# x's transposes shared between DMA and TensorE, and gate and Fourier columns in four equal blocks with the layouts' weighting on VectorE

## The chip, the cores and the metric

The kernel runs on one core of a Trainium2 chip. The metric is device time in microseconds (us), the median of three runs. The profile is of one further execution.

## The reference, cut to what matters

One encoder layer over x (2048 tokens, 1024 columns): RMSNorm, one projection `hn @ w_in` to 6144 columns, split into Fourier columns u_f (512) and their gate g_f (512), queries, keys and values of 24 heads (3 x 1536), and the attention's gate g_a (512).

```python
f = fft2(u_f over sequence and head dim).real @ w_fourier        # per group of 64 columns
y_f = f * silu(g_f)
# three dilated layouts, 8 heads each: o_c and lse_c for layout c
alpha = softmax(stack(lses), axis=0)
y_a = sum(alpha[..., None] * stack(outs), axis=0) * silu(g_a)
y = x + concat([y_f, y_a]) @ w_out
```

q and k are RMS-normed per head, with gains q_norm_w and k_norm_w. The last three lines' weighting (alpha) is "the layouts' weighting" below.

## The kernel before, in words

**Precision.** Each operand of a projection is split into a high and a low fp16 part (index j or l is 0 or 1), and three products of parts are summed, so a product over K = 1024 takes 8 x 3 = 24 matmuls. `xT[:, j, k, token]` holds x transposed, part j.

**The stream of items.** `body` builds a list of items; each is one PSUM tile filled by 24 matmuls. 192 items (`inproj`, L314) are 12 units (layout c, slot pair) times 16 token tiles, with 384 columns of q, k and v. Then come 32 channel items (`chan`, L568, moving 512 tokens: 16 of Fourier gate, 16 of u_f), and 32 token items (`tok`, L582, 256 gate columns for 128 tokens). One loop over i issues item i in slices, and between the slices everything else of that step, by hand: the attention block scheduled for it, the norm of q and k, the weights of the next block, and the output step of the item before (`prev()`). Every engine runs its queue in order, so the place in this loop is the order of work on each engine.

**Weights of a block** (`w_prep`, L254). A block is up to 384 columns. Per block VectorE takes eight maxima (L262), TensorE turns the per-partition maximum round (L268, out 1 x 128), VectorE makes two scale factors on one partition (L270 to L274), TensorE spreads them over 128 partitions (L276, out 128 x 2), and then ScalarE writes the high parts (L291) and VectorE the low parts (L293). There are 17 blocks: 12 units and, by `TSEG`, five in the tail of 384, 384, 256, 256 and 256 columns. `plan` says how many steps of the next block's preparation go into each item.

**The start.** x is loaded by 16 row tiles of 512 KB on SyncE's queue (SP), six buffers. ScalarE sums squares (L191), VectorE takes the reciprocal root (`rsqrt_g`, L103 to L110), ScalarE writes the high part (`x_hi`, L214), VectorE the low part (`x_lo`, L221). Tile 0 is transposed on TensorE (L228), and ScalarE copies the PSUM tiles (L233). Tiles 1 to 15 are transposed by two DMAs each, on SP (`x_dt`, L237). Item 0 of unit 0 needs tile 0, item t needs tile t. Between these, `setup2a` loads both gain tables for all 128 partitions by broadcast (768 KB each, L145 and L146), and `setup2b` makes the combined gains on 128 partitions (GpSimd L158 and L174, VectorE L161 to L171).

**The layouts' weighting** (`og_w`, `og_mul`, `og_add`). The attention writes its outputs with their maxima and sums to DRAM (tile O). For each of 16 groups q of 256 tokens and 256 columns, a load brings all three layouts (792 KB, L634), GpSimd copies maxima and sums out (L647, L648), VectorE makes the weights in eight small steps (L650 to L669) with one exponential on ScalarE (L657), GpSimd multiplies (128 x 1536, L674), and VectorE adds the three layouts (L681, L683). `ga_out` then applies silu (ScalarE L591 and L592, VectorE L593) and multiplies (L693); a token item thus needs its group's sum. The loads start 12 items ahead of the first token item, and the steps run in pace with the token items, one group for two items. ScalarE's silu frees the PSUM tile of a token item, and needs a buffer `ye`, of which there are two, freed by L693.

**Fourier columns** (`u_out`). After every fourth u_f item VectorE and GpSimd fold the sequence into four half-length arrays F (VectorE L619, L622, L623; GpSimd L621, L626, L627).

**The end** (`tail_`). Transposed products with the Fourier map (L746), DFT matmuls (L776), and the output projection (L885) in 16 row tiles. It starts when the last token item's matmuls are done.

Of the kernel before, what the change touches and what calls it, by code (L numbers as in the profile page):

```python
# [23 lines left out]
HD = 64  # L24
# [64 lines left out]
class Kernel:  # L89
# [35 lines left out]
    def setup(self):  # L125
        nc, a, cst = self.nc, self.a, self.cst
        self.idf = cst.tile([128, 128], F32, name="idf")
        make_identity(nc, self.idf)
        self.idh = cst.tile([128, 128], F16, name="idh")
        nc.vector.tensor_copy(self.idh, self.idf)  # L130
        self.ones = cst.tile([1, 128], F32, name="ones")
        nc.vector.memset(self.ones, 1.0)
        self.nw = cst.tile([128, KT], F32, name="nw")
        nc.scalar.dma_start(self.nw, a["norm_w"].rearrange("(k p) -> p k", p=128), allow_slow_non_contiguous=True)
        self.IS = cst.tile([128, 2, 3, 2, 2], F32, name="IS")
        self.dist = self.btp.tile([128, 640], BF16, name="dist")
        self.kf = self.btp.tile([128, 24, HD], F32, name="kf")
        self.bsc = cst.tile([128, 24], F32, name="bsc")
        self.om = cst.tile([128, 24], F32, name="om")
        self.nom = cst.tile([128, 24], F32, name="nom")  # L140

    def setup2a(self):
        nc, a = self.nc, self.a
        kq = self.kq[:, 0].rearrange("p k n -> p (k n)").bitcast(F32).rearrange("p (h d) -> p h d", d=HD)
        nc.sync.dma_start(self.kf, bcast(a["k_norm_w"], 1536))  # L145
        nc.sync.dma_start(kq, bcast(a["q_norm_w"], 1536))  # L146
        nc.sync.dma_start(self.bsc, bcast(a["slopes"], 24))
        nc.sync.dma_start(self.dist, a["dist"])
        self.kqv = kq

    def setup2b(self):
        V = self.nc.vector
        kq = self.kqv
        mx = self.sm.tile([128, 24], F32, name="kmx", bufs=1)
        inv = self.sm.tile([128, 24], F32, name="kinv", bufs=1)
        for i in range(3):
            h = slice(8 * i, 8 * i + 8)
            self.nc.gpsimd.tensor_tensor(self.kf[:, h], self.kf[:, h], kq[:, h], OP.mult)  # L158
        for i in range(3):
            h = slice(8 * i, 8 * i + 8)  # L160
            V.tensor_reduce(mx[:, h], self.kf[:, h], AX.X, OP.max, apply_absolute_value=True)  # L161
            yield
        V.tensor_scalar(mx, mx, 2.0 ** -13, None, op0=OP.max)
        yield
        self.pow2(mx, self.om, inv)
        yield
        V.tensor_scalar(inv, inv, 8.0, None, op0=OP.mult)
        V.tensor_scalar(self.om, self.om, 1.0 / 128, None, op0=OP.mult)
        yield
        V.scalar_tensor_tensor(self.bsc, self.bsc, 8.0, inv, op0=OP.mult, op1=OP.mult)  # L170
        V.tensor_scalar(self.nom, self.om, -1.0, None, op0=OP.mult)  # L171
        for i in range(3):
            h = slice(8 * i, 8 * i + 8)
            self.nc.gpsimd.tensor_tensor(self.kf[:, h], self.kf[:, h], inv[:, h].unsqueeze(2).to_broadcast([128, 8, HD]), OP.mult)  # L174
            yield
# [40 lines left out]
    def x_lo(self, r):  # L216
# [4 lines left out]
        nc.vector.scalar_tensor_tensor(hl[1], t, ri, hl[0], op0=OP.mult, op1=OP.subtract)  # L221
# [9 lines left out]
    def x_ev(self, r, j):  # L231
        E = self.nc.scalar.copy if j or r == 0 else self.nc.vector.tensor_copy
        E(self.xT[:, j, :, r * 128:(r + 1) * 128], self.XP.pop((r, j)))  # L233
# [20 lines left out]
    def w_prep(self, u, nxt=False):  # L254
# [4 lines left out]
        am8 = self.sm.tile([128, KT + 1], F32, name="am8", bufs=2)  # L259
        am = am8[:, KT:KT + 1]  # L260
# [4 lines left out]
        V.tensor_reduce(am, am8[:, :KT], AX.X, OP.max, apply_absolute_value=True)  # L265
# [3 lines left out]
        sc = self.sm.tile([1, 4], F32, name="sc", bufs=2)  # L269
        V.tensor_reduce(sc[:, 2:3], pm[0:1, :128], AX.X, OP.max)  # L270
        V.tensor_scalar(sc[:, 2:3], sc[:, 2:3], 2.0 ** -58, None, op0=OP.max)
        self.pow2(sc[:, 2:3], sc[:, 1:2], sc[:, 0:1])
        V.tensor_scalar(sc[:, 0:1], sc[:, 0:1], 8.0, None, op0=OP.mult)
        V.tensor_scalar(sc[:, 1:2], sc[:, 1:2], 1.0 / 16, None, op0=OP.mult)  # L274
        yield
        nc.tensor.matmul(pm[:, 128:130], self.ones, sc[:, 0:2], start=True, stop=True)  # L276
        sb = self.sm.tile([128, 4], F32, name="scb", tag="scb", bufs=17)
        nws = self.sm.tile([128, KT], F32, name="nws", bufs=2)
        V.tensor_copy(sb[:, 0:2], pm[:, 128:130])
        V.tensor_scalar(nws, self.nw, sb[:, 0:1], None, op0=OP.mult)  # L280
# [294 lines left out]
    def tok(self, u, r):  # L575
# [4 lines left out]
        for k in range(KT):  # L580
            for j, l in ((0, 0), (0, 1), (1, 0)):
                nc.tensor.matmul(ps[:, :256], self.xT[:, j, k, r * 128:r * 128 + 128], wh[:, l, k, :256],  # L582
                                 start=n == 0, stop=n == 23)
                n += 1
                if n % 12 == 0:
                    yield
        self.PS[u, r] = ps
# [7 lines left out]
    def gf_out(self, u, col, ct, ch):  # L595
# [4 lines left out]
        else:  # L600
            t = self.gp.tile([128, 2, 6, UW], F32, name="go", tag="ot", bufs=4).rearrange("p r a w -> p (r a w)")
            o, z = t[:, 0:512], t[:, 512:1024]
# [3 lines left out]
    def u_out(self, u, col, ct, ch):  # L606
        nc = self.nc
        V, G = nc.vector, nc.gpsimd
# [12 lines left out]
        G.tensor_tensor(O[:, 1:1024], U[:, 1:1024], U[:, 2047:1024:-1], OP.subtract)  # L621
# [15 lines left out]
    def og_w(self, q):  # L637
        nc = self.nc
        V, A, G = nc.vector, nc.scalar, nc.gpsimd
        hf, g = divmod(q, 8)  # L640
        ot = self.OT[q]
        T = lambda n, sh: self.sm.tile([128] + sh, F32, name=n, tag=n, bufs=2)
        w, nm, ss = T("cw", [2, 3, 4]), T("cn", [2, 3, 4]), T("cs", [2, 3, 4])
        mn, rc = T("cm", [2, 4]), T("cr", [2, 4])
        fl = lambda x: x.rearrange("p r c (s h) -> p (r c s) h", h=2)
        ov = ot.rearrange("p r a w -> p (r a) w")
        G.tensor_copy(fl(nm), ov[:, :, 130:132])  # L647
        G.tensor_copy(fl(ss), ov[:, :, 128:130])  # L648
# [5 lines left out]
        V.tensor_tensor(w, mn.unsqueeze(2).to_broadcast([128, 2, 3, 4]), nm, OP.subtract)  # L654
        yield
        yield
# [6 lines left out]
        V.tensor_tensor(w, w, iv.unsqueeze(1).to_broadcast([128, 2, 3, 4]), OP.mult)  # L663
# [5 lines left out]
        V.tensor_tensor(w, w, rc.unsqueeze(2).to_broadcast([128, 2, 3, 4]), OP.mult)  # L669
        self.OW[q] = fl(w)  # L670

    def og_mul(self, q):
        O = self.OT[q].rearrange("p r a w -> p (r a) w")[:, :, 0:128].rearrange("p a (h d) -> p a h d", d=HD)
        self.nc.gpsimd.tensor_tensor(O, O, self.OW.pop(q).unsqueeze(3).to_broadcast([128, 12, 2, HD]), OP.mult)  # L674

    def og_add(self, q):
        V = self.nc.vector
        y = self.gp.tile([128, 2, 256], F32, name="yo", tag="yo", bufs=3)
        yv = y.rearrange("p r (s w) -> p r s w", s=2)
        ov = self.OT.pop(q).rearrange("p r (c s) w -> p r c s w", c=3)  # L680
        V.tensor_tensor(yv, ov[:, :, 0, :, 0:128], ov[:, :, 1, :, 0:128], OP.add)  # L681
        yield
        V.tensor_tensor(yv, yv, ov[:, :, 2, :, 0:128], OP.add)  # L683
        self.YO[q] = y

    def ga_out(self, u, hf, r):
        nc = self.nc
        ps = self.PS.pop((u, r))
        q, j = divmod(hf * NT + r, 2)
        y = self.YO[q][:, j]  # L690
        e = self.gp.tile([128, 2, 256], F32, name="ye", tag="ye", bufs=2)
        self.silu(e[:, 0], ps[:, :256], self.W[u][1], e[:, 0], e[:, 1])
        nc.vector.tensor_tensor(y, y, e[:, 0], OP.mult)  # L693
# [200 lines left out]
    TSEG = [[(512, 384)], [(896, 128), (0, 256)], [(256, 256)], [(GAOFF, 256)], [(GAOFF + 256, 256)]]  # L894

    def body(self):
# [3 lines left out]
        with ExitStack() as ctx:  # L900
# [12 lines left out]
            self.YA = drm.tile([S, 512], F32, name="YA")  # L913
            for d in "W WL WS PS RAW QS QR HL TR ST QW VT BT SB PB PH OB OT DT AT OI MX OW XS XR XH XP YO WR XO".split():
# [5 lines left out]
            self.kq = self.wp.tile([128, 2, KT, 384], F16, name="kq", tag="wh", bufs=2)  # L920
# [9 lines left out]
            self.setup2a()  # L930
# [6 lines left out]
            g0 = self.x_rs(0)  # L937
            go(g0, g0, g0, g0, wg, g0, wg, g0, wg, g0, wg, g0, g0, wg, g0, g0)
            for _ in g0:
# [3 lines left out]
            self.x_ev(0, 0)  # L943
            go(wg, wg, wg, wg)
            self.x_lo(0)
            self.x_load(6)
            go(wg)
            self.x_sq(1)
            self.x_tr(0, 1)
            self.x_ev(0, 1)  # L950
            self.x_sq(2)
            go(wg, wg, wg)
# [287 lines left out]
```

## Time and profile before

| | |
|---|---|
| median of 3 runs | 1478.12 us (1477.78 to 1478.91) |
| profiled execution, its own time | 1476.58 us |
| its span, first to last instruction | 1474.8 us |
| mean granted TensorE clock | 0.988 |
| busy: TensorE, VectorE, ScalarE, GpSimd | 1419.4, 1018.1, 744.4, 540.4 us |

PE is TensorE's matmuls, PEld its weight loads, DVE VectorE, ACT ScalarE, POOL GpSimd, SP SyncE, whose queue issues most DMAs. A row of a group reads: line, engine, operation, output<-input, shapes, xcount | busy us, mean ns of one | idle us of the engine just before them, and what ended that idle time. A row of a window reads: start and end, then for each engine its busy us and its number of instructions, then the granted clock (1.00 is full), the DMA engines' busy share and GB/s.

### The profile page before, as it was taken

Reading aid. Unit: us, or ns where it says so; the run is one execution under the profiler, and the core shown is the slowest. Engines: PE = TensorE matmul, PEld = TensorE weight load, DVE = VectorE, ACT = ScalarE, POOL = GpSimd, SP = SyncE. Lnnn points to the kernel's source line nnn. Section 1 sums busy time; section 2 is a strip of 40 time slices with the busy share of each in tenths; the row PEclk is TensorE's granted clock in tenths of the full one; section 3 lists DMA queues with packets and bytes.
Section 4 is the critical chain, followed back from the end, with each engine's and each line's share of the span. In section 5 each row is a group of like instructions: output and inputs, shape, how many; then the busy total and the mean of one; then the engine's idle time right before and its main releaser. Section 6 shows DMA issues by size and latency. Waiting matters only on the chain.

```text
span 1474.8 us, 27958 instructions
## 1 busy us (share of the span) xinstructions
PE 1419.4 (96%) x9466; PEld 1027.9 (70%) x9466; DVE 1018.1 (69%) x3231; ACT 744.4 (50%) x2119; POOL 540.4 (37%) x659
## 2 busy tenths in 40 slices
PE   5899999999999999999999999999998889999999
PEld 2456666667777676678888888644446777878887
DVE  7777888888887887888877787643369995721111
ACT  5666767676756676666666666452222325310000
POOL 1255444444444444444443334310246450411110
PEclk9999999999999999999999999999998999999999
DMA  8987767676776777686746554543214546243332
GB/s 263 219 180 128 144 126 143 126 139 128 142 125 131 136 128 134 124 145 114 149 99 128 105 127 105 131 114 102 73 44 131 182 134 228 101 139 118 108 107 79
DMA packets 425375, 194.66 MB, mean 132 GB/s; under 512 B 321616, under 2 KB 405776, under 8 KB 424720
## 3 DMA queue, kind: packets, MB, share of 16 engines
q1 hardware_dynamic: 424192, 192.87, 58.0%
q8 instruction: 74, 1.21, 0.4%
q14 instruction: 69, 0.57, 0.1%
q10 hardware_dynamic: 1040, 0.00, 0.0%
HBM read 74.17 MB, written 29.75 MB: 70 GB/s over the span
## 4 chain that ended last, share of the span: by engine, by line
PE 69%; DVE 15%; issue 5%; DMA 5%; POOL 4%; ACT 2%; SPq 1%; POOLq 0%; ACTq 0%; DVEq 0%
PE psq L314 35%; PE py L885 12%; PE psq L568 11%; PE pS L463 2%; DMA st<-hl 2%; PE pf L776 2%; PE po L529 2%; POOL ph L511 2%; DVE yo L681 2%; DVE cm L650 1%; DVE qnt L106 1%; DVE wh L293 1%; PE ptr L746 1%; PE pS L451 1%; PE po L530 1%
## 5 line engine op out<-in xcount | busy, mean ns | idle before, releaser
L314 PE MATMUL psq<-wh,xT 128*128 128x384 f16 x4608 | 797.2, 329 | 14.1 <-DMA xT<-xhl 11.4
L314 PEld LDWEIGHTS <-xT 128*128 128x128 f16 x4608 | 541.2, 119 | 215.9 <-issue 16.9
L499 ACT ACTIVATE P<-pS,ob,om 128x256 f32<-128x256 f32 (+1 forms) x384 | 199.6, 527 | 180.7 <-DVE ob L491 180.1
L511 POOL TENSOR_TENSOR ph<-P,ph 128x512 f16<-128x512 f32 x160 | 188.7, 1180 | 189.6 <-ACT ph L506 178.2
L367 POOL TENSOR_TENSOR qn<-qn,kf 128x128 f32<-128x128 f32 x192 | 90.7, 472 | 309.3 <-DVE qn L366 207.9
L885 PE MATMUL py<-wo,mx 128*128 128x512 f32 x768 | 181.3, 395 | 0.3 <-DVE mx L864 0.3
L481 DVE CUSTOM_DVE_ANT_0 pS<-pS,bt 128x256 f32<-128x256 f32 (+1 forms) x384 | 147.6, 384 | 35.0 <-PE pS L451 23.3
L568 PE MATMUL psq<-xT,wh 128*128 128x512 f16 x768 | 169.4, 379 | 0.0
L885 PEld LDWEIGHTS py<-wo,mx 128*128 128x128 f32 x768 | 143.2, 188 | 32.3 <-DVE mx L864 0.8
L378 POOL TENSOR_TENSOR hl<-qn,hl 128x256 f16<-128x256 f32 x192 | 132.9, 692 | 34.0 <-ACT hl L373 34.0
L568 PEld LDWEIGHTS <-wh 128*128 128x128 f16 x768 | 73.7, 98 | 86.9 <-issue 1.4
L888 DVE TENSOR_TENSOR xo<-xo,py 128x512 f32<-128x512 f32 x32 | 22.0, 688 | 139.1 <-PE py L885 139.1
L540 DVE TENSOR_REDUCE ob<-po 128x128 f32<-128x256 f32 (+1 forms) x160 | 75.1, 470 | 44.1 <-PE po L530 44.0
L582 PE MATMUL psq<-wh,xT 128*128 128x256 f16 x768 | 92.5, 285 | 12.5 <-ACT ye L592 8.6
L373 ACT CAST hl<-qn 128x256 f16<-128x256 f32 x192 | 77.1, 401 | 54.3 <-POOL qn L367 47.6
L293 DVE SCALAR_TENSOR_TENSOR wh<-wr,nws,wh 128x384 f16<-128x384 f32 (+1 forms) x136 | 94.7, 704 | 11.8 <-ACT wh L291 11.8
L506 ACT CAST ph<-P 128x512 f16<-128x512 f32 x160 | 99.1, 619 | 5.1
L582 PEld LDWEIGHTS <-xT 128*128 128x128 f16 x768 | 78.2, 102 | 26.7 <-issue 14.5
L333 ACT CAST vt<-psq 128x128 f16<-128x128 f32 x192 | 51.2, 267 | 66.4 <-PE po L530 66.2
L863 ACT CAST mx<-pya 128x512 fp32r<-128x512 f32 x16 | 9.4, 587 | 148.1 <-issue 124.9
L325 ACT COPY raw<-psq 128x256 f32<-128x256 f32 x192 | 69.5, 362 | 26.3 <-PE psq L314 26.0
L334 DVE TENSOR_TENSOR vt<-psq,vt 128x128 f16<-128x128 f32 x192 | 54.9, 286 | 38.1 <-ACT vt L333 37.8
(153 smaller groups left out, 1887.8 us busy)
## 6 DMA issues: line engine op xcount, KB each, us to landing
wr<-in_w_in_dram SPq DMA_DIRECT2D x104, 192.0 KB, 2.8
ot<-O SPq DMA_DIRECT2D x16, 792.0 KB, 4.8
st<-st SPq DMA_DIRECT2D x96, 128.0 KB, 2.4
xs<-in_x_dram SPq DMA_DIRECT2D x16, 512.0 KB, 4.7
xo<-in_x_dram SPq DMA_DIRECT2D x16, 512.0 KB, 3.5
out_dram<-xo SPq DMA_DIRECT2D x15, 512.0 KB, 2.9
O<-ob SPq DMA_DIRECT2D x108, 66.0 KB, 2.4
O<-ob SPq DMA_DIRECT2D x32, 132.0 KB, 2.6
```

The lines of the kernel that those rows point to most:

```text
L293: V.scalar_tensor_tensor(wh[:, 1, k - 1, :n], wr[k - 1], nws[:, k - 1:k], wh[:, 0, k - 1, :n], op0=OP.mult, op1=OP.subtract)
L314: nc.tensor.matmul(ps[:, :384], self.xtile(j, k, c, t), wh[:, l, k, :384], start=n == 0, stop=n == 23)
L367: G.tensor_tensor(qn[:, 2:4], qn[:, 2:4], self.kf[:, h0:h0 + 2], OP.mult)
L373: self.nc.scalar.copy(hl.rearrange("p a h l d -> p (a h) l d")[:, :, 0], qn)
L378: self.nc.gpsimd.tensor_tensor(hv[:, :, 1], qn, hv[:, :, 0], OP.subtract)
L481: V.tensor_tensor_reduce(out=sS[:, h, cs], in0=ps[:, h, cs], in1=bs, scale=1.0, scalar=-3.0e38, op0=OP.add, op1=OP.max, accum_out=mx[:, e, ...
L499: self.nc.scalar.activation(P[:, h, cs], sS[:, h, cs], AF.Exp, bias=ob[:, e, 130 + h:131 + h], scale=self.om[:, h0 + h:h0 + h + 1], accum_ ...
L506: self.nc.scalar.copy(ph[:, 0], P)
L511: self.nc.gpsimd.tensor_tensor(ph[:, 1], P, ph[:, 0], OP.subtract)
L568: nc.tensor.matmul(ps, wh[:, l, k, col * 128:col * 128 + 128], self.xT[:, j, k, ch * 512:ch * 512 + 512], start=n == 0, stop=n == 23)
L582: nc.tensor.matmul(ps[:, :256], self.xT[:, j, k, r * 128:r * 128 + 128], wh[:, l, k, :256], start=n == 0, stop=n == 23)
L885: nc.tensor.matmul(ps[nh], m[:, j, k], wo[nh][k][:, l], start=(j, l, k) == (0, 0, 4), stop=(j, k) == (1, 3))
```

## The change: what it does

1. **Start.** x's high parts (j = 0) of tiles 2 to 15, and both parts of tile 1, are transposed on TensorE, eight 128 x 128 transposes for each tile and part; they are issued in the middle of the item after the one that made them. `x_ev` copies them from PSUM, on ScalarE for tile 0 and where r + j is even, else on VectorE. The low parts of tiles 2 to 15 stay with the DMA, one DMA where there were two. The order of the steps before item 0 is changed.
2. **Gains.** They are worked out on 24 partitions (one head each, VectorE only), written to a small DRAM tile KD and read back by one broadcast load (24 x 67 values for each of 128 partitions) on SP, followed there by the load of `dist`; the small inputs come on ScalarE's DMA queue. `setup2a` and `setup2b` go. The steps run in items 1 and following.
3. **Weights of a block.** The spreading matmul L276 goes: L268 now has the per-partition maximum, broadcast to 128 columns, as its stationary operand, so all 128 partitions get the row of maxima, and VectorE reduces it on all of them. The clamp moves into the maximum (a GpSimd memset of one column).
4. **Blocks.** The tail has four blocks of 384 columns. The third and fourth hold 128 columns of u_f and 256 gate columns each. Tail items in order: 12 and 4 of Fourier gate, 8 and 4 of u_f, 8 token items, 4 of u_f, 8 token items. A token item is now 48 matmuls for 256 tokens.
5. **Weighting ahead, on VectorE.** `og_all` runs through all groups from the sixth step after the attention's end, four small steps per item, two groups' weights at once; the multiplication moves from GpSimd to VectorE. The sums wait in eight buffers `yo`. `ga_out` works on 512 columns at once.
6. **Folding.** The GpSimd steps of `u_out` move to VectorE. The DFT matrix's first load comes with the last u_f item.

```diff
     def x_ev(self, r, j):
-        E = self.nc.scalar.copy if j or r == 0 else self.nc.vector.tensor_copy
+        E = self.nc.scalar.copy if r == 0 or (r + j) % 2 == 0 else self.nc.vector.tensor_copy
     def x_dt(self, r):
-        for j, h in enumerate(self.XH[r]):
-            self.nc.sync.dma_start(self.xT[:, j, :, r * 128:(r + 1) * 128], h, transpose=True)
+        self.nc.sync.dma_start(self.xT[:, 1, :, r * 128:(r + 1) * 128], self.XH[r][1], transpose=True)
...
     def gains(self):
...
+        nc.sync.dma_start(self.KD, kt)
+        src = bass.AP(tensor=self.KD.tensor, offset=self.KD.offset, ap=[[0, 128], [1, 24 * (HD + 3)]])
+        nc.sync.dma_start(self.kb.rearrange("p h d -> p (h d)"), src)
+        nc.sync.dma_start(self.dist, self.a["dist"])
...
     def w_prep(self, u, nxt=False):
...
-        nc.tensor.matmul(pm[0:1, :128], am, self.idf, start=True, stop=True)
...
-        nc.tensor.matmul(pm[:, 128:130], self.ones, sc[:, 0:2], start=True, stop=True)
+        nc.tensor.matmul(pm[:, :128], am.to_broadcast([128, 128]), self.idf, start=True, stop=True)
+        yield
+        V.tensor_reduce(sb[:, 2:3], pm[:, :128], AX.X, OP.max)
...
-    TSEG = [[(512, 384)], [(896, 128), (0, 256)], [(256, 256)], [(GAOFF, 256)], [(GAOFF + 256, 256)]]
+    TSEG = [[(512, 384)], [(896, 128), (0, 256)], [(256, 128), (GAOFF, 256)], [(384, 128), (GAOFF + 256, 256)]]
...
+    def og_all(self):
+        V = self.nc.vector
+        for q in range(2):
+            self.og_load(q)
+        yield
+        for Q in range(8):
+            if Q < 7:
+                self.og_load(2 * Q + 2)
+                self.og_load(2 * Q + 3)
+            yield from self.og_w(Q)
+            for q in (2 * Q, 2 * Q + 1):
...
+                V.tensor_tensor(O, O, self.OW.pop(q).unsqueeze(3).to_broadcast([128, 12, 2, HD]), OP.mult)
+                yield
+                y = self.gp.tile([128, 2, 256], F32, name="yo", tag="yo", bufs=8)
...
+                V.tensor_tensor(yv, ov[:, :, 0, :, 0:128], ov[:, :, 1, :, 0:128], OP.add)
+                yield
+                V.tensor_tensor(yv, yv, ov[:, :, 2, :, 0:128], OP.add)
...
     def body(self):
...
+                if tail and i == AEND + 5:
+                    og = self.og_all()
+                for _ in range(2):
                     next(og, None)
+                while self.YD:
+                    self.ya_st(self.YD.pop(0))
                 if prev:
                     prev()
...
+                for _ in range(2):
+                    next(og, None)
                 next(ip, None)
+                for r in xt:
+                    for j in range(2 if r == 1 else 1):
+                        self.x_tr(r, j)
+                        self.x_ev(r, j)
+                xt = xd
                 for r in xd:
                     self.x_lo(r)
```

More of the change, by code (lines that the diff above doesn't have):

```diff
@@ L151, in setup2b @@
[L151 to L162, printed above, removed]
+        self.kb = self.btp.tile([128, 24, HD + 3], F32, name="kb")
@@ new lines, in setup, with gains @@
+        self.kf = self.kb[:, :, 0:HD]
+        self.bsc, self.om, self.nom = (self.kb[:, :, HD + i] for i in range(3))
+        self.kt = self.sm.tile([24, HD + 3], F32, name="kt", bufs=1)
+        self.kw = self.sm.tile([24, HD], F32, name="kw", bufs=1)
+        nc.scalar.dma_start(self.kt[:, 0:HD], a["k_norm_w"])
+        nc.scalar.dma_start(self.kw, a["q_norm_w"])
+        nc.scalar.dma_start(self.kt[:, HD:HD + 1], a["slopes"].unsqueeze(1))
+    def gains(self):
+        nc, V = self.nc, self.nc.vector
+        kt, kw = self.kt, self.kw
+        mx = self.sm.tile([24, 1], F32, name="kmx", bufs=1)
+        inv = self.sm.tile([24, 1], F32, name="kinv", bufs=1)
+        sl, om, nom = (kt[:, HD + i:HD + i + 1] for i in range(3))
+        V.tensor_tensor(kw, kw, kt[:, 0:HD], OP.mult)
+        yield
+        V.tensor_reduce(mx, kw, AX.X, OP.max, apply_absolute_value=True)
+        yield
@@ L172, in setup2b @@
[L172 to L175, printed above, removed]
+        V.tensor_scalar(sl, sl, inv, 64.0, op0=OP.mult, op1=OP.mult)
+        V.tensor_scalar(nom, om, -1.0 / 128, None, op0=OP.mult)
+        V.tensor_scalar(om, om, 1.0 / 128, None, op0=OP.mult)
+        nc.sync.dma_start(self.KD, kt)
+        src = bass.AP(tensor=self.KD.tensor, offset=self.KD.offset, ap=[[0, 128], [1, 24 * (HD + 3)]])
@@ L258, in w_prep @@
         V, A = nc.vector, nc.scalar
-        am8 = self.sm.tile([128, KT + 1], F32, name="am8", bufs=2)
-        am = am8[:, KT:KT + 1]
+        am8 = self.sm.tile([128, KT + 2], F32, name="am8", bufs=2)
+        am = am8[:, KT + 1:KT + 2]
+        nc.gpsimd.memset(am8[:, KT:KT + 1], 2.0 ** -58)
         for k in range(KT):
@@ L579, in tok @@
         n = 0
[L580 to L587, printed above, removed]
+        for j in range(2):
+            r = q % 8 * 2 + j
+            for k in range(KT):
+                for i, l in ((0, 0), (0, 1), (1, 0)):
+                    nc.tensor.matmul(ps[:, j * 256:j * 256 + 256], self.xT[:, i, k, r * 128:r * 128 + 128],
+                                     wh[:, l, k, 128:384], start=n % 24 == 0, stop=n % 24 == 23)
+                    n += 1
+                    if n % 12 == 0:
+                        yield
+        self.PS[u, q] = ps
     def silu(self, out, ps, sb, e, z):
@@ L668, in og_w @@
         yield
[L669 to L676, printed above, removed]
+        V.tensor_tensor(w, w, rc.unsqueeze(2).to_broadcast([128, 4, 3, 4]), OP.mult)
+        for j in range(2):
+            self.OW[2 * Q + j] = fl(w)[:, 12 * j:12 * j + 12]
@@ L695, in ya_st, with ga_out @@
+    def ga_out(self, u, q):
+        ps = self.PS.pop((u, q))
+        y = self.YO[q].rearrange("p r w -> p (r w)")
+        e = self.gp.tile([128, 2, 512], F32, name="ye", tag="ye", bufs=2)
+        self.silu(e[:, 0], ps, self.W[u][1], e[:, 0], e[:, 1])
+        self.nc.vector.tensor_tensor(y, y, e[:, 0], OP.mult)
+        self.YD.append(q)
     def ya_st(self, q):
@@ L936, in body @@
             self.x_sq(0)
[L937 to L939 removed]
+            go(wg, wg)
+            for _ in self.x_rs(0):
                 pass
@@ L984, in body @@
                 count[it[0]] = count.get(it[0], 0) + 1
-            GA = first.get(U + 3, 1 << 30)
+            UE = first.get(U + 3, 1 << 30) + 4
             prev = None
```

159 lines of the change are left out of this document (57 added, 102 removed).

## The prediction

> **What bounds the kernel now.** I read the page first: the busy tenths of the 40 slices, then the shares of the chain that ended last.
>
> ```profile
> span 1474.8 us, 27958 instructions
> PE   5899999999999999999999999999998889999999
> DVE  7777888888887887888877787643369995721111
> ```
> ```profile
> PE 69%; DVE 15%; issue 5%; DMA 5%; POOL 4%; ACT 2%; SPq 1%; POOLq 0%; ACTq 0%; DVEq 0%
> ```
>
> TensorE is full but for the start and the slices 30 to 32 (counted from 0), and exactly there VectorE is at 9. So a saving counts where TensorE waits, or where work leaves TensorE itself. Next I asked for windows around these two places.
>
> ```profile
> 16.75:44.00 27.25, 20.58 (x69) 8.55 (x69) 23.49 (x65) 15.72 (x28) 7.10 (x6) 0.81 0.87 225
> 44.00:103.00 59.00, 53.42 (x306) 29.98 (x304) 46.06 (x152) 37.40 (x84) 22.46 (x27) 0.94 1.00 201
> 1000.00:1108.00 108.00, 108.00 (x516) 48.94 (x515) 51.75 (x115) 26.33 (x54) 26.79 (x21) 1.00 0.23 71
> 1108.00:1218.00 110.00, 93.71 (x777) 78.89 (x776) 106.96 (x251) 32.16 (x87) 56.77 (x45) 0.92 0.48 149
> ```
>
> The third and fourth rows carry the argument. While the channel items run, VectorE has 56 us to spare and TensorE none. While the token items run, VectorE works 106.96 of 110 us and TensorE idles, at a granted clock of 0.92. Then I looked at what VectorE does there, by groups and shapes over 1000 to 1222 us, and at one place of the timeline.
>
> ```profile
> L582 PE MATMUL psq<-wh,xT 128*128 128x256 f16 x768 | 92.5, 285 | 12.5 <-ACT ye L592 8.6 <-DVE wh L293 3.9
> L674 POOL TENSOR_TENSOR ot<-ot,cw 128x1536 f32<-128x1536 f32 x16 | 48.2, 3012 | 47.8 <-DVE cw L669 47.8
> L681 DVE TENSOR_TENSOR yo<-ot 128x512 f32<-128x512 f32 x16 | 27.3, 1708 | 0.0
> L650 DVE TENSOR_TENSOR cm<-cn 128x8 f32<-128x8 f32 x16 | 20.5, 1283 | 0.0
> L683 DVE TENSOR_TENSOR yo<-yo,ot 128x512 f32<-128x512 f32 x16 | 11.9, 744 | 0.0
> L652 DVE TENSOR_TENSOR cm<-cm,cn 128x8 f32<-128x8 f32 x16 | 2.7, 167 | 0.5
> L732 DVE TENSOR_TENSOR dt<-dr,dt 128x1024 fp32r<-128x1024 f32 x2 | 2.4, 1220 | 0.0
> ```
> ```profile
> 1140.88 3.14 POOL L674 TENSOR_TENSOR ot<-ot,cw 128x1536 f32<-128x1536 f32 x1 [3.53 <-DVE cw L669]
> ```
> ```profile
> 1141.32 2.73 DVE L650 TENSOR_TENSOR cm<-cn 128x8 f32<-128x8 f32 x1
> ```
>
> L650 and L652 have one shape, yet take 1283 and 167 ns; L681 and L683 likewise 1708 and 744. The timeline shows why: L650 begins after GpSimd's multiplication and ends with it (1144.02 and 1144.05 us). So 16 x (1.283 - 0.167) + 16 x (1.708 - 0.744) = 33 of VectorE's 107 us are time in which it stands behind GpSimd.
>
> **The change part by part.** *The gate stage.* The chain of waits gives the pace of TensorE where nothing holds it.
>
> ```profile
> 1000.37 0.45 PE pS L451 x8
> 1000.81 5.18 PE psq L568 x24
> ```
> ```profile
> 1210.13 8.02 PE psq L582 x72
> 1218.15 3.57 PE ptr L746 x32
> ```
> ```profile
> 1108.61 13.26 PE L582 MATMUL psq<-wh,xT 128*128 128x256 f16 x120
> ```
>
> Token matmuls run from 1108.61 to 1218.15, 109.5 us. Unhindered they take 8.02 / 72 = 0.111 us, and 768 of them 85.5 us. The number stays (16 items of 48). So up to 24.0 us is to be had; more than the 12.5 us of idle time in L582's row, since the matmuls after a stall are slow as well. What has to hide VectorE's work now is the time from the sixth step after the attention to the end of the items: 14 channel items x 5.18 + 85.5 = 158 us. Its work there:
> - multiplications: from 744 ns for 512 elements and 1220 for 1024, 0.93 ns an element, so 1.70 us for 1536; 16 make 27 us (GpSimd took 3.01 each);
> - 32 sums at 0.744: 24 us; silu and gate product for 16 items of 512 columns, 32 at 0.744: 24 us;
> - eight small steps for each of eight double groups, 64 at 0.167 (L652): 11 us;
> - folding four columns, each with two operations over 1023 elements (1.22) and four over 512 (0.744), and small copies: 4 x 6 = 24 us;
> - weights of two blocks, at L262 and L293 below: 2 x 8 x (0.55 + 0.73) = 20 us; the DFT matrix, two of L732: 2.4 us.
>
> That is 132 of 158 us, 84%, with nothing from GpSimd in the way but copies of maxima and sums. The cover is thin but there; eight buffers `yo` and three PSUM tiles let VectorE lag by some items. SP's queue gets 16 loads earlier, among the weights' loads; each waits for a buffer that VectorE's sums free, and behind it wait the weights of the last block. TensorE's row has 3.9 us in two waits for a block's weights (L293); I leave one, 2 us. Term: 24 - 2 = **22 us**, bounds 12.5 (the idle time alone) and 24.
>
> *The spreading matmul.* I compared item starts in the chain, and counted the pairs in the answer on tile pm.
>
> ```profile
> 126.11 3.90 PE psq L314 x24
> 130.79 2.92 PE psq L314 x18
> 135.88 2.92 PE psq L314 x18
> 140.97 3.90 PE psq L314 x24
> ```
> ```profile
> L276 PE MATMUL pm<-sc,ones x34: 246/267/369, 14.0 to 1138.1; 1*128 1x2 f32 x34
> ```
>
> A plain item takes 130.79 - 126.11 = 4.68 us; the one with L268 and the one with L276 take 5.09. Each pair costs 0.41 us on a full TensorE. The 34 are 17 pairs, one for each block; two lie in the start, one in the gate stage priced above, so 14 x 0.41 = **5.7 us**. What L268 costs with 128 stationary columns the trace does not show. The nearest row is L746, pairs of the same shape, 3.57 / 16 = 0.22 us back to back, so I take L268 as unchanged; were it twice as dear the term would be 0, and at 0.22 it would be 8.4. The clamp's GpSimd memset runs eight maxima ahead of its reader and costs nothing; GpSimd has half its time free.
>
> *The start.* TensorE begins item 0 at 16.75 and item 15 at 102.90.
>
> ```profile
> 16.75 8.60 PE L314 MATMUL psq<-wh,xT 128*128 128x384 f16 x23 [2.14 <-ACT wh L291]
> ```
> ```profile
> 28.54 0.50 PE L314 MATMUL psq<-wh,xT 128*128 128x384 f16 x1 [2.50 <-DMA xT<-xhl]
> 30.11 6.42 PE L314 MATMUL psq<-wh,xT 128*128 128x384 f16 x23 [1.07 <-DMA xT<-xhl]
> ```
> ```profile
> 102.90 4.06 PE L314 MATMUL psq<-wh,xT 128*128 128x384 f16 x24
> ```
> ```profile
> PE psq L314 <- DMA xT<-xhl: 11.4, 10, 2.5
> ```
> ```profile
> L228 PE MATMUL xps<-idh,xhl 128*128 128x128 f16 x16 | 2.1, 309 | 11.5 <-ACT xhl L214 11.0 <-DVE xhl L221 0.5
> L221 DVE SCALAR_TENSOR_TENSOR xhl<-xs,xri,xhl 128x1024 f16<-128x1024 f32 x16 | 21.6, 1348 | 4.4 <-ACT xhl L214 2.6 <-DMA xT<-xhl 1.9
> L293 DVE SCALAR_TENSOR_TENSOR wh<-wr,nws,wh 128x384 f16<-128x384 f32 x15 | 10.9, 735 | 1.5 <-ACT wh L291 1.5
> L262 DVE TENSOR_REDUCE am<-wr 128x1 f32<-128x384 f32 x16 | 8.5, 547 | 0.2
> L233 ACT COPY xT<-xps 128x1024 f16<-128x1024 f16 x2 | 2.0, 1012 | 1.1 <-PE xps L228 1.1
> ```
>
> Gone: 15 high-part and one low-part DMA transposes of 30, and part of the 11.4 us that TensorE waits for them; after such a wait 23 matmuls took 6.42 us (0.279 each) where a full item takes 3.90, so fewer waits also mean fewer slow matmuls. By the granted clocks, 27.25 x 0.19 + 59 x 0.06 = 8.7 us. Added on TensorE: 16 + 14 x 8 = 128 transposes. They cost 2.1 / 16 = 0.13 us each by L228 (TensorE just started), or 0.056 by the eight 128-column matmuls of L451 at full clock: 16.5 or 7.2 us. So the term lies between 11.4 - 16.5 = -5 and 11.4 + 8.7 - 7.2 = +13. VectorE sets a nearer limit: it gets the copies of tiles 1, 3, to 15, eight at 1.0 to 1.35 us (L233, L221), six of them in the second window, so 46 + 7 = 53 of 59 us are the least there, however fast TensorE is. Against it stands what leaves: reductions and scalings of the gains on 128 partitions. I take the middle, **4 us**.
>
> At this place the Trainium skill speaks against the change: TensorE: Matmul & The Clock Gate, Part 4, gives about 275 to 390 ns for one transposing matmul and says that transposes do not count as activity for the clock gate. By its lower figure 128 transposes would be an estimated 35 us, and the start would lose rather than gain; our two L228 batches ran at 0.13 us apiece, and no run here yet shows them between long matmuls.
>
> *Moved at no cost:* the small inputs on ScalarE's queue, before x's first tile lands; the folding's GpSimd steps, counted above; the tail after 1218 us, where the same work follows. There the DFT matrix's first load still comes three items ahead of its first use.
>
> The sum is 22 + 5.7 + 4 = 31.7. The profiled execution took 1476.58 us (span 1474.8), so it would take 1444.9; the median of the runs lies 1.5 higher, 1478.12, which gives **1446.4 us**.
>
> **The rivals.** *VectorE stays the bound of the gate stage.* Its order is fixed: in each item come four weighting steps, then silu's product, which waits for ScalarE's two passes over 512 columns, then weights. For it: at 84% the waits inside that order may cost the rest. Against it: stalls of 33 us vanish, and the channel items, where VectorE had 56 us free, now carry part of the load. Price: about half the gate stage's term, 12 us, so 1458.
>
> *The gains' round trip holds up SP.* The store to KD must land before the broadcast load goes out, and behind both on SP stand tile 3's low part and the next x load.
>
> ```profile
> st<-st SPq DMA_DIRECT2D x4, 128.0 KB, 3.2
> ```
> ```profile
> kf<-in_k_norm_w_dram SPq DMA_DIRECT2D x1, 768.0 KB, 9.5
> ```
>
> A small copy lands after 3.2 us, a broadcast of this size took 9.5, with the queues full. Item 3 would wait some 7 us and the gain of the start turn into a loss of 3: 1453. For it: the load now falls among x's transposes, where the DMA share is 1.00. Against it: two such loads went out before, and a store of 24 x 67 values is far smaller than the copy in that row.
>
> *The transposes keep TensorE slow* (the side on which the kernel is slower). If the clock stays down while items and transposes alternate, an item takes 24 x 0.279 + 8 x 0.13 = 7.7 us. From 28.5 us, where item 1 began, 14 items end at 136.7 and not at 102.9: 34 us lost against 27.7 gained elsewhere, so 1484. It decides from 7.3 us an item on. Against it: at full clock eight transposes fill 0.45 us, a tenth of an item, and in the window from 44 us, where a tenth of TensorE's time was idle (53.42 busy of 59), the clock was still 0.94. The clock gate's page of the Trainium skill, cited above, is the reason to keep it.
>
> **How the numbers follow.** Forecast 0.65, VectorE as the bound 0.17, the round trip 0.13, slow transposes 0.05. With the terms at their good ends (24, 8.4, and 9 for the start, VectorE's 6 of the second window and 3 of the first) the time is 1437; with one term at its bad end and the others as taken it is 1456 (gate stage), 1452 (spreading) or 1455 (start). So the range 1436 to 1460 holds the forecast and the first two rivals, and leaves out the last and what is left of several bad ends at once. A run of this kernel tells 0.2%, 3 us, from no change. Faster by more gets 0.93, the three faster cases less 0.02 for the first two rivals together at their worst, which is the chance of the same; slower gets the last rival's 0.05.
>
> **What would show it.** Right: token matmuls in about 86 us, VectorE's L681 and L650 near 0.74 and 0.17 us, its tenths near 8 rather than 9 from the first channel item on; one pm pair for each block, and one item of 5.09 us in each unit instead of two; item 15 starting near 99 us; transposes at 0.06 to 0.13 us each. Wrong: TensorE's token matmuls waiting for `ye` or `wh` as before; item 3 waiting for `xT` behind SP's KD store; a granted clock under 0.9 between 44 and 100 us.

## The result, and the profile after

The changed kernel took 1442.47 us (median of 4 runs, 1441.58 to 1443.6) beside 1478.09 for the kernel before on the same chip (1477.78 to 1478.91): ratio 0.9759, interval 0.9742 to 0.9775. Its profiled execution took 1443.6 us, span 1441.8, 33.0 less than before.

From the page of the changed kernel: span, busy tenths of the 40 slices, shares of the chain that ended last.

```profile
span 1441.8 us, 27907 instructions
...
PE   4999999999999999999999999999999999999998
...
DVE  6798888888877888888787777754388675621121
...
PE 73%; DVE 10%; DMA 6%; issue 4%; POOL 4%; ACT 2%; SPq 1%; POOLq 0%; ACTq 0%; DVEq 0%
```

TensorE is at 9 from the second slice to the last but one; the hole of slices 30 to 32 is gone. There VectorE's nines are gone too, and its share of the chain fell from 15 to 10%. The same windows as before, the last two moved with the stages (channel items, then from 1080.50 the token items with four u_f items among them):

```profile
16.75:44.00 27.25, 19.62 (x101) 10.21 (x102) 17.28 (x65) 20.47 (x35) 0.00 (x0) 0.87 0.70 176
44.00:103.00 59.00, 58.66 (x428) 37.38 (x426) 52.99 (x165) 45.29 (x99) 23.10 (x30) 1.00 0.75 165
1000.00:1075.00 75.00, 75.00 (x356) 34.09 (x353) 46.20 (x102) 17.42 (x32) 3.71 (x17) 1.00 0.42 142
1075.00:1190.00 115.00, 115.00 (x934) 91.48 (x933) 85.35 (x162) 33.71 (x58) 7.60 (x18) 1.00 0.35 114
```

In the gate stage TensorE works all 115 us, VectorE 85.35 and GpSimd 7.60, at a granted clock of 1.00 for 0.92. The groups there (965 to 1190 us) answer to the rows of L582, L674, L681, L683 and L650; the small steps now take two groups at once (16 elements for 8):

```profile
L575 PE MATMUL psq<-wh,xT 128*128 128x256 f16 x768 | 84.3, 273 | 0.0
...
L678 DVE TENSOR_TENSOR ot<-ot,cw 128x1536 f32<-128x1536 f32 x16 | 28.0, 1753 | 0.2
...
L683 DVE TENSOR_TENSOR yo<-ot 128x512 f32<-128x512 f32 x16 | 11.1, 691 | 0.4
...
L685 DVE TENSOR_TENSOR yo<-yo,ot 128x512 f32<-128x512 f32 x16 | 11.0, 688 | 0.3
...
L643 DVE TENSOR_TENSOR cm<-cn 128x16 f32<-128x16 f32 x8 | 1.3, 168 | 8.0 <-POOL cn L640 8.0
```

No token matmul has idle time before it. The chain of waits says the same: TensorE alone, item behind item.

```profile
1080.50 3.93 PE psq L575 x36
1084.43 0.22 PE pm L263 x2
1084.66 37.99 PE psq L575 x348
1122.65 20.72 PE psq L559 x96
1143.37 41.92 PE psq L575 x384
1185.29 3.57 PE ptr L748 x32
```

**Where the 33.0 us are.** I cut both spans at three places: item 15's first matmul (102.90 before, 98.65 after), the end of the items that aren't token items, and the first tail matmul (1218.15 and 1185.29).

| part of the span, us | before | after | less by |
|---|---|---|---|
| start, to item 15 | 102.90 | 98.65 | 4.2 |
| item 15 to the last channel item | 1108.61 - 102.90 = 1005.7 | 1080.50 - 98.65 + 20.72 = 1002.6 | 3.1 |
| token items | 1218.15 - 1108.61 = 109.5 | 1185.29 - 1080.50 - 20.72 = 84.1 | 25.5 |
| tail | 1474.8 - 1218.15 = 256.7 | 1441.8 - 1185.29 = 256.5 | 0.1 |

The 20.72 are the four u_f items that now lie among the token items. The 84.1 still hold 0.22 for the last block's pair of matmuls.

### The profile page after: what moved, and what is told of

Read it like the earlier page. It is cut to its first block, busy times and chain, and to the rows that moved or that the text cites. A ratio compares the mean times of both kernels' runs of the same rounds, so it can differ in the third digit from the quotient of the medians.

```text
span 1441.8 us, 27907 instructions
## 1 busy us (share of the span) xinstructions
PE 1402.5 (97%) x9558; PEld 1031.4 (72%) x9558; DVE 989.1 (69%) x3106; ACT 742.3 (51%) x2079; POOL 456.5 (32%) x637
## 4 chain that ended last, share of the span: by engine, by line
PE 73%; DVE 10%; DMA 6%; issue 4%; POOL 4%; ACT 2%; SPq 1%; POOLq 0%; ACTq 0%; DVEq 0%
PE psq L305 33%; PE py L887 12%; PE psq L559 12%; PE psq L575 6%; PE pS L454 2%; PE pf L778 2%; DMA st<-hl 2%; POOL ph L502 2%; PE po L520 2%; DVE qnt L106 1%; DMA pt<-ph 1%; PE ptr L748 1%; POOL hl L369 1%; PE pS L442 1%; PE po L521 1%
## 5 line engine op out<-in xcount | busy, mean ns | idle before, releaser
L490 ACT ACTIVATE P<-pS,ob,kb 128x256 f32<-128x256 f32 (+1 forms) x384 | 199.3, 526 | 187.2 <-DVE ob L482 187.0
L358 POOL TENSOR_TENSOR qn<-qn,kb 128x128 f32<-128x128 f32 x192 | 86.6, 451 | 306.3 <-DVE qn L357 209.5
L284 DVE SCALAR_TENSOR_TENSOR wh<-wr,nws,wh 128x384 f16<-128x384 f32 x128 | 88.6, 697 | 2.9 <-ACT wh L282 2.9
L575 PE MATMUL psq<-wh,xT 128*128 128x256 f16 x768 | 84.3, 273 | 0.0
```

The source lines that it names most:

```text
L284: V.scalar_tensor_tensor(wh[:, 1, k - 1, :n], wr[k - 1], nws[:, k - 1:k], wh[:, 0, k - 1, :n], op0=OP.mult, op1=OP.subtract)
L358: G.tensor_tensor(qn[:, 2:4], qn[:, 2:4], self.kf[:, h0:h0 + 2], OP.mult)
L490: self.nc.scalar.activation(P[:, h, cs], sS[:, h, cs], AF.Exp, bias=ob[:, e, 130 + h:131 + h], scale=self.om[:, h0 + h:h0 + h + 1], accum_ ...
L575: nc.tensor.matmul(ps[:, j * 256:j * 256 + 256], self.xT[:, i, k, r * 128:r * 128 + 128], wh[:, l, k, 128:384], start=n % 24 == 0, stop=n ...
```

## The experiments

"After" is the changed kernel. The kernel before ran beside each, at medians of 1478.03 to 1479.16 us, and ratios are to it.

**The weighting, one half.** In the kernel before, only the engine of the multiplication changes:

```diff
-        self.nc.gpsimd.tensor_tensor(O, O, self.OW.pop(q).unsqueeze(3).to_broadcast([128, 12, 2, HD]), OP.mult)
+        self.nc.vector.tensor_tensor(O, O, self.OW.pop(q).unsqueeze(3).to_broadcast([128, 12, 2, HD]), OP.mult)
```

> The kernel before, with one edit: the layouts' multiplication on VectorE, nothing ahead of time, five blocks as before. Theory (VectorE stood behind GpSimd for 33 us): L681 falls from 1.71 to about 0.69 us and L650 from 1.28 to about 0.17, VectorE gets 16 x 1.75 = 28 us of new work, so the token stage stays VectorE's and shrinks only by about 5 of 109.5 us: 1472 to 1475. Rival (the long rows are VectorE's own cost): 28 us come on top and the stage takes about 137 us: about 1505.

Measured: 1468.69 us, ratio 0.9932 (0.9917 to 0.9947). Groups and one window of this kernel:

```profile
L582 PE MATMUL psq<-wh,xT 128*128 128x256 f16 x768 | 88.1, 277 | 6.3 <-ACT ye L592 4.5 <-DVE wh L293 1.8
```
```profile
1108.00:1210.00 102.00, 90.78 (x783) 77.40 (x781) 97.75 (x269) 32.68 (x87) 14.72 (x30) 0.97 0.53 163
```

VectorE took on 28 us of multiplications and the kernel still gained some 10 (1479.16 beside it), more than I expected: L681 and L650 fell to 683 and 158 ns in this run, from 1708 and 1283. So VectorE really had stood behind GpSimd. But it still works 97.75 of 102 us, and TensorE still waits.

**The other half.** In after, the multiplication goes back to GpSimd (the reverse edit), and stays ahead of the token items.

> The changed kernel with the multiplication back on GpSimd, all else as changed, still ahead of time. Theory (room ahead of the token items decides as much as the engine): VectorE now waits about 3 us for each multiplication just ahead of its sum, 16 x 3 = 48 us in place of 28 of work, so it needs some 150 of 158 us and TensorE waits for little: 1443 to 1455. Rival (the engine is what decides): nearly all of the 25 us that the stage gained are lost, 1463 to 1468.

Measured: 1442.94 us, ratio 0.9758 (0.9744 to 0.9773): no loss. Groups of this kernel, 965 to 1190 us:

```profile
L575 PE MATMUL psq<-wh,xT 128*128 128x256 f16 x768 | 84.3, 273 | 0.0
...
L678 POOL TENSOR_TENSOR ot<-ot,cw 128x1536 f32<-128x1536 f32 x16 | 47.8, 3005 | 89.1 <-DVE cw L660 78.7 <-DVE am L259 10.4
L683 DVE TENSOR_TENSOR yo<-ot 128x512 f32<-128x512 f32 x16 | 23.7, 1479 | 11.2 <-POOL ot L678 8.3 <-DMA YA<-yo 2.9
```

The sums are slow again (1479 ns for 691), and it costs nothing, because VectorE has room for it. Windows from the first load of the weighting to the tail's first matmul, in after and in this kernel:

```profile
1022.17:1185.12 162.95, 162.95 (x1131) 110.71 (x1130) 117.14 (x230) 41.67 (x74) 10.90 (x33) 1.00 0.39 131
```
```profile
1021.39:1184.35 162.96, 162.96 (x1132) 110.79 (x1131) 112.89 (x211) 41.40 (x74) 65.49 (x49) 1.00 0.40 130
```

The slow sums are less work for VectorE than the multiplications that left it (112.89 us for 117.14). So the change of engine by itself is worth 10 us, and all the rest of the stage's change without it is worth the whole term. That rest is more than the earlier start: two groups' weights at once, four blocks in place of five and silu on 512 columns are in it as well. No run takes them apart, so that the earlier start alone would do is not shown.

**How thin the cover is.** The weighting begins six items later, with three steps at a time for two:

```diff
-                if tail and i == AEND + 5:
+                if tail and i == AEND + 11:
...
-                for _ in range(2):
+                for _ in range(3):
...
-                for _ in range(2):
+                for _ in range(3):
```

> The changed kernel, with the weighting started six items later and six steps an item in place of four: VectorE's work must fit 24 items (about 126 us) in place of 30. Theory (about 15% spare over 158 us): it now needs 90 to 95% of its time and TensorE waits a little: 1443 to 1450. Rival (the thin cover of the prediction is real and any delay shows at once): about 30 us of work lose their cover, 1455 to 1470.

Measured: 1440.69 us, ratio 0.9743 (0.9729 to 0.9758). Neither expectation held: nothing was lost, and the token matmuls again run in unbroken stretches of 37.99 and 41.92 us. The 1.8 us less lie ahead of this stage (item 15 starts at 96.79), where this kernel doesn't differ. So two kernels with the same instructions there can lie 2 us apart, and a difference of that size need be no effect of an edit.

**The transposes.** All of x on TensorE (no DMA transposes), and, in a second kernel, both parts of tiles 2 to 15 by DMA as before:

```diff
-                for r in xd:
-                    self.x_dt(r)
...
-                    for j in range(2 if r == 1 else 1):
+                    for j in range(2):
```
```diff
-        self.nc.sync.dma_start(self.xT[:, 1, :, r * 128:(r + 1) * 128], self.XH[r][1], transpose=True)
+        for j, h in enumerate(self.XH[r]):
+            self.nc.sync.dma_start(self.xT[:, j, :, r * 128:(r + 1) * 128], h, transpose=True)
...
-                    for j in range(2 if r == 1 else 1):
+                    for j in range(2 if r == 1 else 0):
```

> The changed kernel with the low parts of x transposed on TensorE too, no transposing DMA of x. Theory (0.055 us a transpose, clock full): 112 more cost TensorE 6.2 us; item 2 no longer waits 3.4 us for a DMA; VectorE and ScalarE get 14 more copies of 0.7 to 1.0 us in a stage where VectorE is 90% busy: 3 to 8 us more, 1445 to 1450. The clock gate's page of the Trainium skill (TensorE: Matmul & The Clock Gate, Part 4) gives 275 ns a transpose and a clock that transposes don't raise: an estimated 31 us more, 1473.

> The changed kernel with both parts of x's tiles 2 to 15 transposed by DMA again (tile 1 still on TensorE). Theory (the transposes' move is what brought the start its 4 us): item 15 starts at 102 to 104 us in place of 98.7, about 1446. Rival (the start's gain came from the gains' new way and tile 1 alone): item 15 within 1 us of the changed kernel, 1442 to 1443.

Measured: 1447.16 us for the first (ratio 0.9783, 0.9766 to 0.9799), 1446.11 for the second (0.9784, 0.9771 to 0.9797), 4.7 and 3.6 us above after. Item 15 starts at 105.92 and 102.55; the forecast for the second held, and the first lost as little as the trace, not the Trainium skill, had it. So half and half is better than either whole; each end has its own wait, as TensorE's waits from 0 to 103 us show. The first kernel's, on VectorE's copies out of PSUM:

```profile
PE xps L223 <- DVE xT L228: 4.8, 1, 4.8
```

The second's, on the transfers, as in the kernel before:

```profile
PE psq L306 <- DMA xT<-xhl: 12.6, 15, 3.4
```

After itself has one such wait, of item 2 for its low part, and one for item 0's weights (same view):

```profile
PE psq L305 <- ACT wh L282: 4.9, 1, 4.9
PE psq L305 <- DMA xT<-xhl: 3.4, 1, 3.4
```

**After once more,** for its scatter.

> The changed kernel itself, as the measure for the three that run beside it: 1441 to 1444.

Measured: 1442.57 us (1441.6 to 1443.75), ratio 0.976 (0.9746 to 0.9773). But item 0 starts at 18.71 and item 15 at 97.35 where the first profile had 19.68 and 98.65: single places of the start scatter by a microsecond. By this second profile (token items from 1080.47, tail from 1185.25) the table's first two rows give 5.6 and 1.9 in place of 4.2 and 3.1, and the token items 25.5 as before: what the gate stage gained is sure; what the start and the stretch behind it gained is sure only as a sum.

**The spreading matmul.** The two matmuls of the kernel before are put back into after, with the small steps on one partition between them.

```diff
-        nc.tensor.matmul(pm[:, :128], am.to_broadcast([128, 128]), self.idf, start=True, stop=True)
+        nc.tensor.matmul(pm[0:1, :128], am, self.idf, start=True, stop=True)
...
+        nc.tensor.matmul(pm[:, 128:130], self.ones, sc[:, 0:2], start=True, stop=True)
```

> The changed kernel with the scale factors made on one partition and spread by a second matmul again (L268 and L276 as before). In the trace the round cost two items 0.41 us each before, and one item 0.22 us after. Theory A (TensorE sets the pace of all units): 14 x 0.60 = 8.4 us more, about 1451. Theory B (in the units of the second layout other waits fill what TensorE saves, as the idle time before the pS matmuls on tile qw suggests, 4.6 us before and 7.5 after): only some 8 to 10 blocks count and 3 to 5 us are lost, 1445 to 1447.

Measured: 1446.1 us (1445.19 to 1448.28), ratio 0.9787 (0.9774 to 0.98), 3.6 over after. TensorE's waits from 103 to 1000 us explain why it isn't 8, first in after:

```profile
PE pS L454 <- DMA qw<-qw: 7.5, 9, 1.3
PE pm L263 <- DVE am L260: 3.4, 3, 1.4
PE po L520 <- DMA pt<-ph: 1.5, 4, 0.8
```

and in this kernel:

```profile
PE pS L457 <- DMA qw<-qw: 4.7, 7, 1.0
PE pm L263 <- DVE am L260: 1.8, 3, 0.8
PE po L523 <- DMA pt<-ph: 0.3, 1, 0.3
```

The waits are 6.8 us here; in after 13.1 with two small ones not shown, and 9.9 to 14.3 in the other kernels with one matmul. Of the 8.4 us that after saves TensorE in 14 blocks, it spends 6.3 in longer waits, 2.8 of them for the attention's q tiles (`qw`) to land.

**Four edits at the start** of after. The copy of tile 0's first part goes ahead of the squares of tiles 1 and 2 on ScalarE:

```diff
+            self.x_ev(0, 0)
-            self.x_sq(1)
...
-            self.x_sq(2)
-            self.x_ev(0, 0)
...
             self.x_ev(0, 1)
+            self.x_sq(1)
+            self.x_sq(2)
```

> The changed kernel with ScalarE's copies of x's tile 0 ahead of the squares of tiles 1 and 2, which wait for loads. In the changed kernel item 0 starts at 19.7 us, 2.9 us later than before the change. Theory A (the delay goes through to the end): about 1439.5. Theory B (item 2 waits for its low part, whose DMA stands behind the next block's weights, whenever item 0 starts): item 0 starts near 17 us, the wait of 3.4 us grows, and the time stays within 1 us.

The second block's weight loads go behind x's transposes on SP:

```diff
-                    if u == 0 and p < 2:
-                        for k in range(4 * p, 4 * p + 4):
-                            self.w_load(1, k)
...
                     self.x_dt(r)
+                if i in (1, 2):
+                    for k in range(4 * i - 4, 4 * i):
+                        self.w_load(1, k)
```

> The changed kernel with the loads of unit 1's weights one item later and behind the low part of x's tile in SP's order (items 1 and 2 in place of 0 and 1). Theory (item 2 waits 3.4 us for a low part whose DMA was issued behind eight weight loads): the wait goes, item 2 starts at about 34 us, and 2 to 3 us arrive at item 15 and at the end: about 1440. Rival (VectorE's pace in the following items takes it back): item 15 as before within 1 us, 1442.

KD's store, its broadcast load and `dist` go to GpSimd's queue:

```diff
-        nc.sync.dma_start(self.KD, kt)
+        nc.gpsimd.dma_start(self.KD, kt)
...
-        nc.sync.dma_start(self.kb.rearrange("p h d -> p (h d)"), src)
-        nc.sync.dma_start(self.dist, self.a["dist"])
+        nc.gpsimd.dma_start(self.kb.rearrange("p h d -> p (h d)"), src)
+        nc.gpsimd.dma_start(self.dist, self.a["dist"])
```

> The changed kernel with the gains' store and broadcast load, and the load of dist, on GpSimd's DMA queue. In the changed kernel they hold SP from 35.4 to 38.6 us, while tile 3's low part was ready at 34.9 and ScalarE later stands 6.9 us for an x load. Theory (this round trip is the rival of the prediction and costs something): item 15 starts 2 to 3 us sooner, about 1440. Rival (no later step of TensorE depends on it, as TensorE's waits show none): within 1 us, 1442.

The three small input loads go from ScalarE's queue to SP's, behind x's tile 5:

```diff
-        nc.scalar.dma_start(self.kt[:, 0:HD], a["k_norm_w"])
-        nc.scalar.dma_start(self.kw, a["q_norm_w"])
-        nc.scalar.dma_start(self.kt[:, HD:HD + 1], a["slopes"].unsqueeze(1))
...
             for r in (4, 5):
                 self.x_load(r)
+            nc.sync.dma_start(self.kt[:, 0:HD], self.a["k_norm_w"])
+            nc.sync.dma_start(self.kw, self.a["q_norm_w"])
+            nc.sync.dma_start(self.kt[:, HD:HD + 1], self.a["slopes"].unsqueeze(1))
```

> The changed kernel with the three small loads of gains and slopes off ScalarE's queue and on SP, behind the first six loads of x. In the changed kernel SP's weight loads stand 2.7 us at this place, and x's tile 1 lands late for ScalarE, whose queue holds the squares of tiles 1 and 2 ahead of item 0's weights. Theory: item 0 starts at 17 to 18 us in place of 19.7; how much of the 2 us reaches the end tells whether the front of the start sets its end: 1440 to 1441 if it does, 1442 if item 2's wait for a DMA takes it back.

Measured: 1442.46 us (ratio 0.9759, 0.9745 to 0.9772), 1443.95 (0.977, 0.9757 to 0.9784), 1441.87 (0.9756, 0.9743 to 0.977) and 1439.9 (1438.95 to 1440.26; 0.9742, 0.9729 to 0.9755). The first missed its aim: item 0 started at 19.16, inside the scatter, since the squares still lay ahead of the weights' high parts on ScalarE; it tells nothing. The second took away item 2's wait, and item 3 then waited 4.61, so nothing arrived at the end. The third shows the round trip all but free: its median is 0.6 under after's. (Its item 15 starts at 96.58, as early as in the kernel with the late weighting, whose start is the same as after's, so this is scatter.) The fourth gained 2.6 us, and its range lies clear of after's. So does the range of the kernel with the late weighting, 1.8 lower without an edit at the start. The size of the gain is therefore not settled, but its way is seen on SP's queue and in SP's waits of the first 12 us, first in after:

```profile
1.19 6.67 SPq L241 DMA_DIRECT2D wr<-in_w_in_dram  x8
```
```profile
SPq L241 <- DMA nw<-in_norm_w_dram: 2.7, 1, 2.7
```

and in the fourth:

```profile
1.19 5.22 SPq L238 DMA_DIRECT2D wr<-in_w_in_dram  x8
```
```profile
SPq L238 <- DMA nw<-in_norm_w_dram: 0.2, 1, 0.2
```

With the three small loads (12 KB in all) on ScalarE's queue, SP takes 1.45 us longer to issue the first block's weights, and x's tile 1 behind them goes out as much later (7.91 for 6.45). The single issues take 0.4 to 0.5 us each. SP stands 2.7 us before the fourth of the eight, until `nw`, the first load on ScalarE's queue, has landed at 5.36. In this program the loads of both queues tell of their landing by eight semaphores in turn, so the ninth load waits for the first; the three small ones take three of the eight, and SP comes to the ninth load sooner. In the fourth kernel it is the seventh weight load that waits for `nw`. (Its sixth issue takes 1.5 us there; why is not settled.) The other copies of after with those loads on ScalarE took 6.44 to 6.67 there, the kernels without them 5.22 to 5.49. In the fourth kernel item 0 starts at 17.45 and item 15 at 95.94.

**One step further:** in the fourth kernel, tile 2's low part on TensorE too.

```diff
                 for r in xd:
-                    self.x_dt(r)
+                    if r > 2:
+                        self.x_dt(r)
-                    for j in range(2 if r == 1 else 1):
+                    for j in range(2 if r < 3 else 1):
```

> Edit: the three small loads behind x's tile 5 on SP's queue, as in the run before, and the low part of x's tile 2 transposed on TensorE as well (eight transposes of some 0.055 us and one copy more, one DMA transpose less on SP), so that item 2 waits for no DMA. In the run before this one item 2 waited 3.04 us for that transfer and item 3 then 0.61, and the median was 1439.9. Theory (TensorE's chain sets the end from item 0 on, and what a tile gains at the start arrives): most of the 3 us is gone, less 0.44 for the transposes and perhaps 1 for the copy, item 15 starts 1.5 to 3 us sooner than in the run before, median 1437 to 1438.5. Rival (the transfers and norms of the tiles behind it are late anyway, item 3's transposed low part and the tile loads above all, so the wait moves one or two items on): PE's waits for xT add up to about the same in items 3 to 7, median 1439.5 to 1440.5.

Measured: 1439.33 us (1438.09 to 1442.0), ratio 0.9743 (0.9729 to 0.9756), the same as without it. The rival holds: item 2 runs through, and the wait stands one item on, as TensorE's timeline of this kernel shows (item 15 starts at 97.14).

```profile
34.15 2.43 PE L302 MATMUL psq<-wh,xT 128*128 128x384 f16 x13
41.18 3.70 PE L302 MATMUL psq<-wh,xT 128*128 128x384 f16 x11 [4.59 <-DMA xT<-xhl]
```

## Why the prediction was right, point by point

The forecast was 1446.4 us, the measured time 3.9 less. By the profiles the terms were 31.7 and came to 33.0, which is 1.3 of it. The other 2.6 lie in where the profiled executions fell: 1.5 under the median before, 1.1 over the median after.

**The gate stage, 22 us: it gave 25.5.** VectorE, full in this stage, held TensorE. Its stall behind GpSimd was a part of that, worth some 10 us by the first experiment; L681 fell to 0.69 us, and L650's step to 0.17. The multiplication took 1.753 us, 1.70 by the working. Two things were too cautious. The 2 us kept back for a block's weights didn't come: no token matmul waited. And the 768 matmuls took 83.8 us (3.93 + 37.99 + 41.92), not 85.5, 0.109 each and not the 0.111 of the one row that I used. What I had not seen is that the change of engine could stay away: I priced it and the head start as one, and called a cover of 84% thin. In the window above VectorE is busy 117.14 of 162.95 us, 72%, and six items less of cover changed nothing. The first rival (VectorE stays the bound) fell with that.

**The spreading matmul, 5.7 us: it gave 3.1,** by two errors against each other. L263 with 128 stationary columns wasn't as dear as L268; a plain item and one with a pair, in the chain of after:

```profile
127.23 2.92 PE psq L305 x18
130.16 0.22 PE pm L263 x2
130.38 0.97 PE psq L305 x6
...
132.13 3.90 PE psq L305 x24
```

From 127.23 to 132.13 are 4.90 us against 136.81 - 132.13 = 4.68 for the plain item behind it, so the pair costs 0.22, the good end of my bounds, and 14 blocks before against 13 in the same stretch after (the tail has one less) could give 14 x 0.82 - 13 x 0.22 = 8.6. The failing step is "full TensorE": it waited 13.1 us between 103 and 1000 after, 8.5 before (4.6 + 3.3 + 0.6 in the same view), so 4.6 of it went into longer waits, nearly all on transfers. The prediction took no account of these waits; a saving on a busy engine arrives only where nothing else is just on time. That leaves 0.9 of the 8.6 without a name, within the scatter. The edit's worth by profiles is smaller than by medians: the two-matmul kernel's profiled span is 1443.4 us, only 1.6 over after's, and its medians are 3.6 apart (the profiled execution was the fastest of that kernel's five and the slowest of after's four); both lie under 5.7.

**The start, 4 us: it gave 4.2,** though not along my path. Item 0 starts 2.9 us later (19.68 for 16.75). Most of it is the small loads on ScalarE's queue, which I had put at no cost, and which make SP wait 2.7 us before a weight load: in the two kernels without them there it starts at 17.45 and 17.21, in the others at 18.28 to 19.68. Item 2 waits 3.4 us, and behind that wait the granted clock is 0.50, as this window of after shows.

```profile
37.60:42.00 4.40, 4.40 (x20) 2.54 (x21) 0.00 (x0) 1.12 (x1) 0.00 (x0) 0.50 0.74 206
```

Then the items run at full pace: in the window from 44 us the clock is 1.00 and VectorE works 52.99 us. That this is the 53 of my bound is luck: the six copies in it take 4.1 us, not 7, and other work fills the rest. From item 0 to item 15 it takes 79.0 us for 86.2. The experiments with tile 2's low part and with the second block's loads show why the 3.4 us are no gain waiting to be had: take them away, and item 3 waits 4.6 instead. What makes item 3's low part late then isn't settled; in both kernels its transposing DMA went out behind KD's load and `dist`, and the two were not tried with those on another queue.

**The gains' round trip** (rival, 0.13) costs next to nothing: on GpSimd's queue the time is 0.6 us less, within the scatter, and in after SP waits 1.9 us for KD while item 2 is waiting anyhow.

**The transposes keep TensorE slow** (rival, 0.05) fell. Eight transposes lie between an item's halves:

```profile
30.74 0.61 PE L223 MATMUL xps<-idh,xhl 128*128 128x128 f16 x8
31.18 2.11 PE L305 MATMUL psq<-wh,xT 128*128 128x384 f16 x12
```

They hold TensorE 31.18 - 30.74 = 0.44 us, 0.055 each, the lower end I had from L451, and the granted clock of the window from 44 us is 1.00. The Trainium skill, TensorE: Matmul & The Clock Gate, Part 4, gives 275 to 390 ns and says that transposes don't count as activity for the gate. Here, as `nc.tensor.transpose` issued eight at a time between long matmuls, they cost a fifth of the lower figure, and the clock stays; even at a granted clock of 0.50, in the batch at 41.09 behind item 2's wait, eight take 0.85 us, 0.106 each. With all 256 on TensorE, 16 between two items, the clock is 1.00 too from 60 to 103 us; whether a long run of transposes alone would keep it up, no run here shows. In that kernel item 15 starts 7.3 us later than in after: 14 x 8 more at 0.055 are 6.2, the wait for VectorE's copy 4.8, and item 2's 3.4 is gone. Of the 7.3 the median shows 4.7. The lower figure of the Trainium skill, TensorE: Matmul & The Clock Gate, Part 4, would have made the 112 alone an estimated 31 us.

## What to carry to other kernels

When one engine stands behind another's long instructions, moving the work off the other engine and giving it more room are two separate cures; try each alone, since here the first by itself gave 10 us, and the rest of the change was enough without it. A saving on the engine that is always busy is worth its price less what was just on time behind it, so read that engine's waits in the same stretch first. Where several waits stand one behind the other, as in this start, taking one away names the next.

## What the runs showed of the hardware

Small loads on one engine's queue can hold up another's: with the 12 KB above on ScalarE's queue SP needed 6.67 us for eight issues in place of 5.22, because it stood 2.7 us for the landing of a load there. VectorE takes a transposed tile out of PSUM sooner than ScalarE, as the groups of after between 44 and 103 us show:

```profile
L228 ACT COPY xT<-xps 128x1024 f16<-128x1024 f16 x6 | 6.1, 1014 | 0.0
L228 DVE COPY xT<-xps 128x1024 f16<-128x1024 f16 x6 | 4.1, 682 | 0.0
```

Its share of the copies is thus cheaper than the 1.0 to 1.35 us that I had put. The quickest kernels here, the fourth start edit and the one with tile 2 as well, take 1439.9 and 1439.3 us, some 3 less than the change as given, of which up to 2 can be scatter.
